# Attention's values as a seventh group of the mixers, second sums by adding transfers, one projection woven in

## The chip, the cores and the metric

The kernel runs on one core of a Trainium2 chip. The metric is the device time of one execution in microseconds (us); lower is better. The core's engines each run a queue of instructions in order: TensorE (PE: matmuls; PEld: its weight loads), VectorE (DVE), ScalarE (ACT), GpSimd (POOL) and SyncE (SP). SP, ACT and POOL also issue the transfers (DMAs).

## The reference

An encoder block over 256 tokens, width 2048, all in float32: a half-step gated FFN, then two token mixers in parallel, merged by gates, then a second half-step FFN and a norm. The part that matters here:

```python
h = rmsnorm(x, norm_mix_g[l])
proj = h @ w_in[l]
q_a, k_a, v_a, q_r, k_r, v_r, g_r, gate_a, gate_r = jnp.split(proj, IN_SPLIT_POINTS, axis=-1)
att = chunked_band_attention(q_a, k_a, v_a, rel_bias[l])       # 8 heads of 128, softmax
branch_a = att @ w_out_att[l]
ret = chunkwise_retention(rotary(q_r), rotary(k_r), v_r)       # 8 heads of 128, decay
branch_r = (silu(g_r) * ret) @ w_out_ret[l]
merged = sigmoid(gate_a) * branch_a + sigmoid(gate_r) * branch_r
x = x + merged @ w_out[l]
```

(The reshapes to heads are left out.) q_a, k_a, v_a, q_r, k_r, v_r and g_r are 1024 wide, the two gates 2048.

## The kernel before

**Matmuls.** Every product of activations and weights is made of three matmuls. Weights come as blocks of 256 rows by 512 columns in float32 (`raw`, 512 KB, on SP's queue). `split` makes a high part of a block on ScalarE (L140) and a low part on VectorE (L141); `three` multiplies high by high (L151), by the activations' low part (L152) and low by high (L154). Four pairs of split tiles go round, so a block's split can start when TensorE is through with the block four steps earlier.

**Steps.** The program is one list of steps; a step splits one block and multiplies it. A *standard* step (S below) serves both halves of the 256 tokens: 2 row pieces x 2 halves x 3 = 12 matmuls. A projection of 512 columns is 8 of them. `run` writes the instructions of all engines step by step; splits are written up to four steps ahead, and `later(n, fn)` puts other work n steps on. Each engine then keeps the order in which it was written.

**Groups.** The class `Strassen` makes two blocks of 512 columns at once with seven products instead of eight, from sums of blocks of the weights and of the activations. A group is 28 steps of 6 matmuls, in phases 0 to 3; for each of four row blocks jc there is a step r of a block itself and a step s of a sum (phase 3 has s only). A step's tiles are named by group, phase, jc and kind: `hiz49502s` is the high part of group z495, phase 0, jc 2, the sum. The order of the steps is 0r0 0r1 0s0 0r2 0s1 0r3 0s2 0s3 in phase 0, the same in phases 1 and 2, then 3s0 to 3s3.

The sums of weights live in two tiles per jc, `k` (kept) and `x`, both loaded on POOL's queue (L540). The *first* sum x + k is made on VectorE (L529); with `MIX_ADDED = (0,)` that of jc 0 is made by an adding transfer from k to x (L545) in all groups of the mixers but the first. The *second* sum adds the raw block of phase 1 to x, on VectorE in the step 1r (L597). The *third* replaces k by x - k on VectorE (L583), and x gets another block of weights added by a transfer from memory on POOL's queue (L584). That queue carries, in this order, the next group's loads, the third sums of this one, and so on, and each third sum waits until x has been split and k replaced.

**The mixers.** `weave` puts standard steps between the steps of the groups, at a rate worked out from their number and the shares in `MIX_SHARE`. The groups are attention's queries (`qa`, z390), the gates in four groups, and retention's gate (`gr`, z565); the projections woven in are attention's keys KA and values VA and retention's values VR, two each. Queries, keys and values go to memory and are brought back for the heads (`bring_back`). After the last group, at step `mixed`, follow the standard steps of retention's QR0, KR0, QR1 and KR1; the eight heads of attention are put between them at `HEAD_AT`, and retention's heads after each KR. Then branch a's and branch r's output projections, `w_out`, and the second FFN.

`ret_qk_done` takes QR or KR from its banks (ACT, tile `qr`), rotates it on VectorE in six operations per half of the tokens (`turn`, L905 to L908), transposes it on TensorE (`qr0p`, L368) and copies it out. `ROTATED` says how many steps after the projection's last step the two transposes stand.

Of the kernel before, what the change touches and what calls it, by code (L numbers as in the profile page):

```python
# [41 lines left out]
RET_WAIT = (14, 6)  # L42
RET_PUT = ((3, 5), (2, 2))
HELD = 6
MIX_ADDED = (0,)
FIRST_ADDED = (2, 3)
MIX_AHEAD = 12
FIRST_WAIT = 4
LAST_SUM = 24
ROTATED = {("q", 0): (6, 7), ("k", 0): (5, 6), ("q", 1): (4, 5), ("k", 1): (3, 4)}  # L50
HEAD_AT = (3, 6, 10, 13, 17, 20, 24, 27)

MIX_SHARE = (0.5,) * 4 + (1.0,) * 4 + (0.0,) * 4 + (0.2,) * 4
SHARE = (0.75,) * 4 + (1.0,) * 4 + (0.0,) * 4 + (0.2,) * 4
# [32 lines left out]
def block_kernel(ctx: ExitStack, tc: tile.TileContext, x, g1, w1g, w1u, w1d, gm, w_in, rel, woa, wor, wo,  # L87
# [419 lines left out]
    class Strassen:  # L507
# [3 lines left out]

        def __init__(self, norm, w1, col1, w2, col2, evict, added=()):
            self.added, self.summed = added, set()
            self.add_wait, self.early = ADD_WAIT, False
            self.norm, self.w, self.col, self.evict = norm, (w1, w2), (col1, col2), evict
            self.x, self.kept, self.acc, self.wide = {}, {}, {}, {}
            self.name = f"z{len(steps)}"
# [52 lines left out]
        def step(self, phase, jc, of_sum):  # L570
# [4 lines left out]
            def load():  # L575
                made["raw"] = weights_tile(f"raw{name}")
                i = 2 - phase
                fetch(made["raw"], self.w[i], self.rows(1, jc), self.col[i])

            def third():  # L580

                x, k = self.x[jc], self.kept[jc]
                nc.vector.tensor_sub(k, x, k)  # L583
                nc.gpsimd.dma_start(x, chunk(self.w[0], self.rows(1, jc), self.col[0]), accum_op=ALU.add)  # L584

            def prep():
                x = self.x[jc]
                if not of_sum:
                    if phase == 0:
                        made["w"] = split(self.kept[jc], name)  # L590
                        if jc not in self.added and not self.early:
                            self.first_once(jc)
                        return
                    raw = made.pop("raw")
                    made["w"] = split(raw, name)
                    if phase == 1:
                        nc.vector.tensor_add(x, x, raw)  # L597
                elif phase == 2:
                    made["w"] = split(self.kept.pop(jc), name)
                elif phase == 3:  # L600
                    made["w"] = split(self.x.pop(jc), name)
                else:
                    if phase == 0:
                        self.first_once(jc)
                    made["w"] = split(x, name)
                    if phase == 1:
                        third()

# [77 lines left out]
    def weave(jobs, apart, groups, lead, share, start=None, extra=0, ahead=8):  # L686
# [18 lines left out]
        for _ in range(lead):  # L705
            next_standard()
        seconds = []
        rate = (len(queue) - apart) / (len(groups) * sum(share))
        credit = 0.0
        first = max(len(steps) - ahead, D // NB)  # L710
        for n, (b, make) in enumerate(groups.items()):
            group = make()
            group.added = FIRST_ADDED if n == 0 and start is not None else group.added[:n]
            if n == 0 and start is not None:
                group.add_wait = 2
            group.early = n == 0 and ahead > 8
            loads = group.loads()
            if start is not None and n == 0:
                loads[0] = lambda load=loads[0]: [start(), load()]
            kept.extend((first + i if n == 0 else 0, fn) for i, fn in enumerate(loads))  # L720
            for i, part in enumerate(group.steps()):
                if i == HALF_K // KC + 2:
                    seconds.append(len(steps))
                steps.extend(part)
                credit += rate * share[i]
                if i + 1 == len(share):
                    at_hand[b] = len(steps) + 7

                turn = i + 1 == 3 * (HALF_K // KC)
                if (turn or credit >= (0.2 if (i + 1) % (HALF_K // KC) == 0 else 0.6)) and next_standard():  # L730
                    credit -= 1
# [159 lines left out]
    def ret_qk_done(key, b, after=None):  # L891
        def done(acc):
            srcs = []
            half = HD // 2

            def turn(t, s):
                r = tmp_tile(f"{key}{b}{t}r", "qk", 4)
                u = tmp_tile(f"{key}{b}{t}u", "scaled", 1)
                s4 = s.rearrange("p (h j d) -> p h j d", h=4, j=2)
                r4 = r.rearrange("p (h j d) -> p h j d", h=4, j=2)  # L900
                u4 = u.rearrange("p (h j d) -> p h j d", h=4, j=2)
                c = cos_sb[:, t, :].unsqueeze(1).to_broadcast([P, 4, half])
                n = sin_sb[:, t, :].unsqueeze(1).to_broadcast([P, 4, half])
                for j in range(2):
                    nc.vector.tensor_mul(r4[:, :, j, :], s4[:, :, j, :], c)  # L905
                    nc.vector.tensor_mul(u4[:, :, j, :], s4[:, :, 1 - j, :], n)
                nc.vector.tensor_sub(r4[:, :, 0, :], r4[:, :, 0, :], u4[:, :, 0, :])
                nc.vector.tensor_add(r4[:, :, 1, :], r4[:, :, 1, :], u4[:, :, 1, :])  # L908
                srcs.append(r)


            for t in range(NT):
                s = tmp_tile(f"{key}{b}{t}", "gate", 2)
                nc.scalar.activation(s, acc[t], AF.Copy, scale=nm.scale(t))
                later(1 + t, lambda t=t, s=s: turn(t, s))
            to_transposed(key, b, srcs, ROTATED[key[0], b])
            if after is not None:
                after()

        return done  # L920
# [17 lines left out]
    def attention(h):  # L938
# [53 lines left out]
            hi, lo = att.alloc(b)  # L992
            split_out(ps[:, :SEQ], hi[:, i, :], lo[:, i, :])

        return (0, scores), (1, powers), (2, shares), (4, transposes), (6 + (h < HEADS - 2), values)

    def all_attention():
        for h in range(HEADS):
# [77 lines left out]
    def gates(col1, col2, func, dsts):  # L1076


        def evict(t, side, r):
            if side == 1:  # L1080
                nc.scalar.activation(r, r, func)
            else:
                bank, r = r, tmp_tile(f"sg{col1}{t}", "gate", 2)
                nc.scalar.activation(r, bank, func, scale=nm.scale(t))
# [10 lines left out]
    def queries():  # L1095
# [9 lines left out]

        return Strassen(nm, w_in0, QA, w_in0, QA + NB, evict, MIX_ADDED)

    groups = {"qa": queries, **groups}
    weave(
        [proj(KA + b * NB, att_qk_done("ka", b), both) for b in range(2)]  # L1110
        + [proj(VA + b * NB, nat_done("va", b, AF.Copy), both) for b in range(2)]
        + [proj(VR + b * NB, nat_done("vr", b, AF.Copy), both) for b in range(2)],
        0, groups, MIX_LEAD, MIX_SHARE, None, EXTRA, MIX_AHEAD,
    )
    mixed = len(steps)
    for b in range(2):
        add([proj(QR + b * NB, ret_qk_done("qr", b)), proj(KR + b * NB, ret_qk_done("kr", b, lambda b=b: retention(b)))])

    merged = Operand("mg", D // NB)
    def load_gates(name, src):  # L1120
# [129 lines left out]
    mix = next(c for c, s in enumerate(steps) if s.job.w is w_in0)  # L1250
    at(mix - 18, load_rel)
    at(mix - 18, lambda: later(4, load_gain(gm, 1)))
    at(mixed - 6, set_bias)
    at(mixed - 3, lambda: bring_back(0))
    at(mixed + 5, lambda: bring_back(1))
    at(mixed, all_attention)
    at(merges[0][0] + 4, lambda: later(9, load_gain(g2, 2)))
    at(mixed + 16, load_ret_gates)
    at(mixed + 20, set_decay)
    for step, fn in merges:  # L1260
        at(step - 8, fn)

# [63 lines left out]
```

## Time and profile before

| what | value |
|---|---|
| median of 3 runs | 2037.34 us (2037.06 to 2037.85) |
| the profiled execution | 2037.64 us, its span 2035.9 us |
| TensorE busy | 99% |
| VectorE, ScalarE, GpSimd busy | 88%, 74%, 17% |
| moved by DMA | 504.77 MB, mean 248 GB/s |

Busy means that an instruction of the engine was under way. The mixers' groups run from 708 to 1054 us, the standard steps with the heads from there to 1159, the second FFN's first group starts at 1380 us. In lists of groups of instructions each row has line, engine, operation, tiles written and read, shape, count, and busy time; in timelines a row begins with its start and its length.

### The profile page before, as it was taken

What the parts mean: (1) busy time and instruction counts of PE and PEld (TensorE: products, weight loads), DVE (VectorE), ACT (ScalarE), POOL (GpSimd) and SP (SyncE); (2) the same over time, 40 slices, a digit from 0 to 9 for tenths busy, and PEclk for the clock granted to TensorE, in tenths of its full rate; (3) what the DMA queues carried; (4) which work ended last, traced back from release to release, by engine and by line L of the source; (5) the groups of instructions that cost most, each with busy time, mean ns of one, the idle gap of its engine ahead of it and who ended that gap; (6) DMA issues with size and microseconds to landing.
All of it is one profiled execution on the core that took longest, in us unless ns stands there. A gap on an engine that the chain in (4) does not pass through costs nothing.

```text
span 2035.9 us, 26220 instructions
## 1 busy us (share of the span) xinstructions
PE 2023.9 (99%) x9170; PEld 1678.8 (82%) x9170; DVE 1786.5 (88%) x1823; ACT 1504.3 (74%) x1886; POOL 342.9 (17%) x399
## 2 busy tenths in 40 slices
PE   9999999999999999999999999999999999999998
PEld 7788888888888888888888888888888888888886
DVE  7999999999998898999987677569999999999996
ACT  7788888878888777777765434557788888888885
POOL 1221122212112021111120000011112221122200
PEclk9999999999999999999999999999999999999999
DMA  9888899988878689899897645576889988889974
GB/s 311 255 249 258 255 269 281 262 240 250 260 235 237 218 232 303 273 283 286 256 320 236 209 156 185 186 247 188 263 268 276 274 243 237 258 269 270 285 199 135
DMA packets 226436, 504.77 MB, mean 248 GB/s; under 512 B 15776, under 2 KB 16480, under 8 KB 226304
## 3 DMA queue, kind: packets, MB, share of 16 engines
q1 hardware_dynamic: 154560, 297.31, 43.1%
q0 software_dynamic: 67536, 196.80, 37.4%
q10 hardware_dynamic: 4208, 8.99, 1.2%
q8 instruction: 72, 1.18, 0.2%
q14 instruction: 60, 0.49, 0.1%
HBM read 471.04 MB, written 10.50 MB: 237 GB/s over the span
## 4 chain that ended last, share of the span: by engine, by line
PE 98%; DVE 0%; DMA 0%; ACT 0%; issue 0%; POOL 0%; DVEq 0%; POOLq 0%; ACTq 0%; SPq 0%
PE acc L152 15%; PE acc L151 15%; PE acc L154 15%; DMA raw<-in_ffn_w_gate_dram 0%; PE z298a L152 0%; PE z530a L151 0%; PE z425a L151 0%; PE z850a L152 0%; PE z154a L152 0%; PE z1030a L152 0%; PE z994a L152 0%; PE z565a L151 0%; PE z742a L152 0%; PE z334a L152 0%; PE z118a L152 0%; PE z886a L152 0%
## 5 line engine op out<-in xcount | busy, mean ns | idle before, releaser
L141 DVE TENSOR_TENSOR lo<-raw,hi 128x1024 fp32r<-128x1024 f32 x351 | 427.7, 1221 | 118.7 <-ACT hi L140 113.8
L140 ACT CAST hi<-raw 128x1024 fp32r<-128x1024 f32 x351 | 368.0, 1050 | 178.0 <-PE acc L152 134.0
L808 ACT ACTIVATE xall<-acc 128x512 f32<-128x512 f32 x160 | 94.6, 591 | 13.4 <-PE acc L154 9.3
L805 ACT ACTIVATE acc<-xall 128x512 f32<-128x512 f32 x160 | 95.9, 600 | 2.5
L151 PE MATMUL acc<-hi,mgh 128*128 128x512 f32 x128 | 50.2, 392 | 0.0
L152 PE MATMUL acc<-hi,mgl 128*128 128x512 f32 x128 | 49.8, 389 | 0.0
L154 PE MATMUL acc<-lo,mgh 128*128 128x512 f32 x128 | 35.5, 390 | 0.0
L151 PE MATMUL acc<-hi,nma01h 128*128 128x512 f32 x80 | 32.0, 400 | 0.0
L151 PE MATMUL acc<-hi,nma00h 128*128 128x512 f32 x80 | 31.9, 398 | 0.0
L152 PE MATMUL acc<-hi,nma01l 128*128 128x512 f32 x80 | 31.2, 390 | 0.0
L152 PE MATMUL acc<-hi,nma00l 128*128 128x512 f32 x80 | 31.2, 390 | 0.0
L151 PE MATMUL acc<-hi,nma11h 128*128 128x512 f32 x80 | 31.2, 390 | 0.0
L151 PE MATMUL acc<-hi,nma10h 128*128 128x512 f32 x80 | 31.2, 390 | 0.0
L152 PE MATMUL acc<-hi,nma11l 128*128 128x512 f32 x80 | 31.2, 390 | 0.0
L152 PE MATMUL acc<-hi,nma10l 128*128 128x512 f32 x80 | 31.2, 390 | 0.0
L154 PEld LDWEIGHTS acc<-lo,mgh 128*128 128x128 f32 x128 | 24.0, 188 | 5.0
L151 PEld LDWEIGHTS acc<-hi,mgh 128*128 128x128 f32 x128 | 24.0, 188 | 4.9
L152 PEld LDWEIGHTS acc<-hi,mgl 128*128 128x128 f32 x128 | 24.1, 188 | 4.8
L151 PE MATMUL acc<-hi,atth 128*128 128x512 f32 x64 | 25.7, 402 | 0.0
L151 PE MATMUL acc<-hi,reth 128*128 128x512 f32 x64 | 25.3, 395 | 0.0
L359 POOL TENSOR_TENSOR n2rstd<-v,mhalf 128x2 f32<-128x2 f32 x1 | 0.7, 695 | 144.6 <-DVE v L358 144.6
L152 PE MATMUL acc<-hi,attl 128*128 128x512 f32 x64 | 25.0, 390 | 0.0
(6885 smaller groups left out, 7279.9 us busy)
## 6 DMA issues: line engine op xcount, KB each, us to landing
raw<-in_ffn_w_down_dram SPq DMA_DIRECT2D x176, 512.0 KB, 7.1
raw<-in_w_in_dram SPq DMA_DIRECT2D x80, 512.0 KB, 5.7
raw<-in_w_out_dram SPq DMA_DIRECT2D x32, 512.0 KB, 3.7
raw<-in_ffn_w_up_dram SPq DMA_DIRECT2D x16, 512.0 KB, 4.9
raw<-in_w_out_att_dram SPq DMA_DIRECT2D x16, 512.0 KB, 3.9
raw<-in_w_out_ret_dram SPq DMA_DIRECT2D x16, 512.0 KB, 3.7
raw<-in_ffn_w_gate_dram SPq DMA_DIRECT2D x15, 512.0 KB, 4.9
z390x<-in_w_in_dram POOLq DMA_DIRECT2D x8, 512.0 KB, 8.8
```

The lines of the kernel that those rows point to most:

```text
L140: nc.scalar.copy(hi, raw)
L141: nc.vector.tensor_sub(lo, raw, hi.bitcast(F32))
L151: nc.tensor.matmul(acc, ahi, whi, start=first, stop=False, **more)
L152: nc.tensor.matmul(acc, alo, whi, start=False, stop=False, **more)
L154: nc.tensor.matmul(acc, ahi, wlo, start=False, stop=last, **more)
L359: nc.gpsimd.tensor_tensor(dst, v, mhalf[:, :width], op=ALU.pow)
L805: nc.scalar.activation(acc, xs[t][:, cols], AF.Copy, scale=2.0)
L808: nc.scalar.activation(xs[t][:, cols], acc, AF.Copy, scale=0.5)
```

## The change

1. Attention's values become a group of the mixers, after the queries (`va`, z425): VA's two projections leave the list of standard steps, and the group's results go to memory half by half.
2. The second sums of jc 1 to 3 of every group of the mixers are made by adding transfers from memory on POOL's queue (`second`, L582 of the new file), after the sum's split in phase 0, ahead of the third sums. The one of jc 0 stays on VectorE.
3. The first sum of jc 0 is made on VectorE in all groups of the mixers (`MIX_ADDED = ()`).
4. QR0 is woven in as the last projection; after the mixers follow KR0, QR1 and KR1 only. The first group gets half as many standard steps again as the others (`fuller`).
5. The heads stand closer (`HEAD_AT`), the transposes of QR and KR at other steps (`ROTATED`), the rotations in another order and with a tile of their own, and the loads that go with them at other steps.

```diff
-MIX_ADDED = (0,)
+MIX_ADDED = ()
+SECOND_WAIT = 1
-ROTATED = {("q", 0): (6, 7), ("k", 0): (5, 6), ("q", 1): (4, 5), ("k", 1): (3, 4)}
-HEAD_AT = (3, 6, 10, 13, 17, 20, 24, 27)
+ROTATED = {("q", 0): (3, 4), ("k", 0): (4, 7), ("q", 1): (4, 7), ("k", 1): (3, 4)}
+HEAD_AT = (1, 4, 6, 9, 12, 14, 17, 20)
...
+            def second():
+                nc.gpsimd.dma_start(self.x[jc], chunk(self.w[1], self.rows(1, jc), self.col[1]), accum_op=ALU.add)
...
-                    if phase == 1:
+                    if phase == 1 and jc not in self.seconds:
                         nc.vector.tensor_add(x, x, raw)
...
                     made["w"] = split(x, name)
+                    if phase == 0 and jc in self.seconds:
+                        later(SECOND_WAIT, second)
...
-        rate = (len(queue) - apart) / (len(groups) * sum(share))
+        fuller = 0.5 if ahead > 8 else 0.0
+        rate = (len(queue) - apart) / ((len(groups) + fuller) * sum(share))
...
+            if ahead > 8:
+                group.seconds = range(1, HALF_K // KC)
...
-                for j in range(2):
+                for j, op in enumerate((ALU.subtract, ALU.add)):
+                    u = tmp.tile([P, NB // 2], F32, tag="turned", name=f"{key}{b}{t}u{j}", bufs=1)
                     nc.vector.tensor_mul(r4[:, :, j, :], s4[:, :, j, :], c)
-                    nc.vector.tensor_mul(u4[:, :, j, :], s4[:, :, 1 - j, :], n)
-                nc.vector.tensor_sub(r4[:, :, 0, :], r4[:, :, 0, :], u4[:, :, 0, :])
-                nc.vector.tensor_add(r4[:, :, 1, :], r4[:, :, 1, :], u4[:, :, 1, :])
+                    nc.vector.tensor_mul(u3, s4[:, :, 1 - j, :], n)
+                    nc.vector.tensor_tensor(r4[:, :, j, :], r4[:, :, j, :], u3, op=op)
...
-    groups = {"qa": queries, **groups}
+    def va_values():
+        return gates(VA, VA + NB, AF.Copy, [by_tokens(to_dram["va"][b]) for b in range(2)])
+
+    groups = {"qa": queries, "va": va_values, **groups}
     weave(
         [proj(KA + b * NB, att_qk_done("ka", b), both) for b in range(2)]
-        + [proj(VA + b * NB, nat_done("va", b, AF.Copy), both) for b in range(2)]
-        + [proj(VR + b * NB, nat_done("vr", b, AF.Copy), both) for b in range(2)],
+        + [proj(VR + b * NB, nat_done("vr", b, AF.Copy), both) for b in range(2)]
+        + [proj(QR, ret_qk_done("qr", 0), both)],
         0, groups, MIX_LEAD, MIX_SHARE, None, EXTRA, MIX_AHEAD,
     )
```

In the program, the groups of the mixers are z390, z425, z460, z495, z530 and z565 before, with 7 standard steps in each; they are z390, z425, z458, z491, z523, z556 and z588 after, with 7, 5, 5, 4, 5, 4 and 4. In phase 0 the last five have no standard step before the end of the phase; before, one stood after 0r2 and one after 0s3.

**Start of a group on VectorE.** Phase 0 of the fourth group before (`lo499` is a standard step's low part; L529 a first sum):

```order
L141 TENSOR_TENSOR loz49500r_7815<-z495k0_7305,hiz49500r_7814 128x1024
L141 TENSOR_TENSOR loz49501r_7825<-z495k1_7665,hiz49501r_7824 128x1024
L529 TENSOR_TENSOR z495x1_7696<-z495x1_7696,z495k1_7665 128x1024
L141 TENSOR_TENSOR loz49500s_7838<-z495x0_7323,hiz49500s_7837 128x1024
L141 TENSOR_TENSOR loz49502r_7848<-z495k2_7722,hiz49502r_7847 128x1024
L529 TENSOR_TENSOR z495x2_7734<-z495x2_7734,z495k2_7722 128x1024
L141 TENSOR_TENSOR lo499_7863<-raw499_7639,hi499_7862 128x1024
L141 TENSOR_TENSOR loz49501s_7875<-z495x1_7696,hiz49501s_7874 128x1024
L141 TENSOR_TENSOR loz49503r_7887<-z495k3_7758,hiz49503r_7886 128x1024
L529 TENSOR_TENSOR z495x3_7770<-z495x3_7770,z495k3_7758 128x1024
L141 TENSOR_TENSOR loz49502s_7898<-z495x2_7734,hiz49502s_7897 128x1024
```

and of the fourth group after (L142 is the low part, L530 the first sum):

```order
L142 TENSOR_TENSOR loz49100r_7734<-z491k0_7267,hiz49100r_7733 128x1024
L530 TENSOR_TENSOR z491x0_7285<-z491x0_7285,z491k0_7267 128x1024
L142 TENSOR_TENSOR loz49101r_7745<-z491k1_7584,hiz49101r_7744 128x1024
L530 TENSOR_TENSOR z491x1_7615<-z491x1_7615,z491k1_7584 128x1024
L142 TENSOR_TENSOR loz49100s_7758<-z491x0_7285,hiz49100s_7757 128x1024
L142 TENSOR_TENSOR loz49102r_7768<-z491k2_7641,hiz49102r_7767 128x1024
L530 TENSOR_TENSOR z491x2_7653<-z491x2_7653,z491k2_7641 128x1024
L142 TENSOR_TENSOR loz49101s_7783<-z491x1_7615,hiz49101s_7782 128x1024
L142 TENSOR_TENSOR loz49103r_7793<-z491k3_7677,hiz49103r_7792 128x1024
L530 TENSOR_TENSOR z491x3_7689<-z491x3_7689,z491k3_7677 128x1024
L142 TENSOR_TENSOR loz49102s_7806<-z491x2_7653,hiz49102s_7805 128x1024
```

The standard step's low part is gone, and a first sum of jc 0 stands in the second place.

**QR0's rotation on VectorE, after.** Phase 2 of the last group (L654 is the group's combination of two banks, `qr00` and `qr01` the two halves of QR0, L914 to L916 the rotations):

```order
L142 TENSOR_TENSOR loz58822r_9332<-rawz58822r_9216,hiz58822r_9331 128x1024
L654 SCALAR_TENSOR_TENSOR z588c12_9308<-z588c_9088,nmminus_92,z588c12_9308 128x512
L914 TENSOR_TENSOR qr00r_9338<-qr00_9326,cos_sb_80 128x4x64
L915 TENSOR_TENSOR qr00u0_9339<-qr00_9326,sin_sb_81 128x256
L916 TENSOR_TENSOR qr00r_9338<-qr00r_9338,qr00u0_9339 128x4x64
L914 TENSOR_TENSOR qr00r_9338<-qr00_9326,cos_sb_80 128x4x64
L915 TENSOR_TENSOR qr00u1_9343<-qr00_9326,sin_sb_81 128x256
L916 TENSOR_TENSOR qr00r_9338<-qr00r_9338,qr00u1_9343 128x4x64
L142 TENSOR_TENSOR loz58821s_9354<-z588k1_8878,hiz58821s_9353 128x1024
L914 TENSOR_TENSOR qr01r_9357<-qr01_9328,cos_sb_80 128x4x64
```

and the same place on TensorE (L155 is a product with a low part, `acc90` QR0's banks, L369 the transposes):

```order
L155 MATMUL acc90_1_8745<-lo607_9267,nma11h_6114 128x512 x2
L155 MATMUL z588b_9129<-loz58820r_9285,nma01h_6110 128x512 x2
L155 MATMUL z588b_9129<-loz58821r_9297,nma01h_6110 128x512 x2
L369 MATMUL qr0p0_9378<-id_sb_78,qr00r_9338 128x128 x4
L155 MATMUL z588a_9065<-loz58820s_9311,nms7h_6366 128x512 x2
L369 MATMUL qr0p1_9396<-id_sb_78,qr01r_9357 128x128 x4
L155 MATMUL z588b_9129<-loz58822r_9332,nma01h_6110 128x512 x2
```

(The products with high parts between these rows are left out.) Between QR0's last matmul and the first transposes stand two steps of a group, 2r0 and 2r1, and one more between the transposes. Before, they stood behind standard steps of KR0, six and seven steps after QR0's last.

**POOL's queue**, from a group's third sums to the next group's, before (L545 is the first sum of jc 0 by transfer):

```order
L540 DMA z530x0_7805<-in_w_in_dram 128x2x512
L545 DMA z530x0_7805<-z530k0_7787 128x1024
L584 DMA z495x0_7323<-in_w_in_dram 128x2x512
L584 DMA z495x1_7696<-in_w_in_dram 128x2x512
L584 DMA z495x2_7734<-in_w_in_dram 128x2x512
L584 DMA z495x3_7770<-in_w_in_dram 128x2x512
```

and after (L582 the second sums, L588 the third):

```order
L541 DMA z523x0_7724<-in_w_in_dram 128x2x512
L582 DMA z491x1_7615<-in_w_in_dram 128x2x512
L582 DMA z491x2_7653<-in_w_in_dram 128x2x512
L582 DMA z491x3_7689<-in_w_in_dram 128x2x512
L588 DMA z491x0_7285<-in_w_in_dram 128x2x512
L588 DMA z491x1_7615<-in_w_in_dram 128x2x512
L588 DMA z491x2_7653<-in_w_in_dram 128x2x512
L588 DMA z491x3_7689<-in_w_in_dram 128x2x512
```

Seven adding transfers stand where five stood.

More of the change, by code (lines that the diff above doesn't have):

```diff
@@ L513, in __init__ @@
             self.added, self.summed = added, set()
-            self.add_wait, self.early = ADD_WAIT, False
+            self.add_wait, self.early, self.seconds = ADD_WAIT, False, ()
             self.norm, self.w, self.col, self.evict = norm, (w1, w2), (col1, col2), evict
@@ L724, in weave @@
                 steps.extend(part)
-                credit += rate * share[i]
+                credit += rate * share[i] * (1 + (fuller if n == 0 else 0))
                 if i + 1 == len(share):
@@ L897, in turn @@
                 r = tmp_tile(f"{key}{b}{t}r", "qk", 4)
-                u = tmp_tile(f"{key}{b}{t}u", "scaled", 1)
                 s4 = s.rearrange("p (h j d) -> p h j d", h=4, j=2)
                 r4 = r.rearrange("p (h j d) -> p h j d", h=4, j=2)
-                u4 = u.rearrange("p (h j d) -> p h j d", h=4, j=2)
                 c = cos_sb[:, t, :].unsqueeze(1).to_broadcast([P, 4, half])
                 n = sin_sb[:, t, :].unsqueeze(1).to_broadcast([P, 4, half])
-                for j in range(2):
+                for j, op in enumerate((ALU.subtract, ALU.add)):
+                    u = tmp.tile([P, NB // 2], F32, tag="turned", name=f"{key}{b}{t}u{j}", bufs=1)
+                    u3 = u.rearrange("p (h d) -> p h d", h=4)
                     nc.vector.tensor_mul(r4[:, :, j, :], s4[:, :, j, :], c)
-                    nc.vector.tensor_mul(u4[:, :, j, :], s4[:, :, 1 - j, :], n)
-                nc.vector.tensor_sub(r4[:, :, 0, :], r4[:, :, 0, :], u4[:, :, 0, :])
-                nc.vector.tensor_add(r4[:, :, 1, :], r4[:, :, 1, :], u4[:, :, 1, :])
+                    nc.vector.tensor_mul(u3, s4[:, :, 1 - j, :], n)
+                    nc.vector.tensor_tensor(r4[:, :, j, :], r4[:, :, j, :], u3, op=op)
                 srcs.append(r)
@@ L993, in values @@
             split_out(ps[:, :SEQ], hi[:, i, :], lo[:, i, :])
-        return (0, scores), (1, powers), (2, shares), (4, transposes), (6 + (h < HEADS - 2), values)
+        return (0, scores), (1, powers), (2, shares), (4, transposes), (6, values)
     def all_attention():
@@ L1080, in evict @@
             if side == 1:
-                nc.scalar.activation(r, r, func)
+                if func != AF.Copy:
+                    nc.scalar.activation(r, r, func)
             else:
@@ L1116, in block_kernel @@
     for b in range(2):
-        add([proj(QR + b * NB, ret_qk_done("qr", b)), proj(KR + b * NB, ret_qk_done("kr", b, lambda b=b: retention(b)))])
+        jobs = [proj(QR + b * NB, ret_qk_done("qr", b)), proj(KR + b * NB, ret_qk_done("kr", b, lambda b=b: retention(b)))]
+        add(jobs if b else jobs[1:])
     merged = Operand("mg", D // NB)
@@ L1252, in block_kernel @@
     at(mix - 18, lambda: later(4, load_gain(gm, 1)))
-    at(mixed - 6, set_bias)
-    at(mixed - 3, lambda: bring_back(0))
-    at(mixed + 5, lambda: bring_back(1))
+    at(mixed - 8, set_bias)
+    at(mixed - 6, lambda: bring_back(0))
+    at(mixed + 2, lambda: bring_back(1))
     at(mixed, all_attention)
     at(merges[0][0] + 4, lambda: later(9, load_gain(g2, 2)))
-    at(mixed + 16, load_ret_gates)
-    at(mixed + 20, set_decay)
+    at(mixed + 12, load_ret_gates)
+    at(mixed + 14, set_decay)
     for step, fn in merges:
```

## The prediction

> **What bounds the kernel now.** I read the page first: the busy times and the chain that ended last.
>
> ```profile
> span 2035.9 us, 26220 instructions
> PE 2023.9 (99%) x9170; PEld 1678.8 (82%) x9170; DVE 1786.5 (88%) x1823; ACT 1504.3 (74%) x1886; POOL 342.9 (17%) x399
> PE 98%; DVE 0%; DMA 0%; ACT 0%; issue 0%; POOL 0%; DVEq 0%; POOLq 0%; ACTq 0%; SPq 0%
> ```
>
> TensorE is the chain. So a matmul removed is worth its own pace, and every new wait of TensorE costs its full length. The pace comes from the timeline of one mixer group (z495, the fourth), whose first matmul and the next group's first are
>
> ```profile
> 883.26 0.39 PE L151 MATMUL z495a<-hiz49500r,nma00h 128*128 128x512 f32 x1
> 940.38 0.39 PE L151 MATMUL z530a<-hiz53000r,nma00h 128*128 128x512 f32 x1
> ```
>
> The 0.39 us is how long one takes, not how often one starts: between the rows lie 28 group steps of 6 matmuls and 7 standard steps of 12, that is 252, in 57.12 us. One starts every 0.2267 us; a group step is 1.36 us, a standard step 2.72 us. Nothing is left in those 57 us for a wait.
>
> Who could make TensorE wait is read from the windows (second number of each pair in brackets: instructions; last two columns: share of the DMA engines, GB/s) and from the waits.
>
> ```profile
> 883.20:940.40 57.20, 57.20 (x254) 47.35 (x254) 54.25 (x49) 41.83 (x46) 11.60 (x13) 1.00 0.92 281
> 860.00:880.00 20.00, 20.00 (x90) 16.57 (x89) 17.79 (x17) 15.72 (x17) 7.05 (x9) 1.00 1.06 348
> 1020.00:1040.00 20.00, 20.00 (x90) 16.57 (x89) 20.00 (x19) 12.97 (x13) 7.82 (x10) 1.00 1.03 247
> 1040.00:1060.00 20.00, 20.00 (x90) 16.58 (x89) 13.77 (x13) 15.41 (x19) 0.53 (x1) 1.00 1.04 396
> ACT hi L140 <- PE acc L152: 134.0, 87, 3.9
> DVE lo L141 <- ACT hi L140: 113.8, 99, 3.8
> ```
>
> In a group VectorE is busy 54.25 of 57.20 us and the DMA engines 0.92. ScalarE (41.83 us) has room: its largest idle is the wait for TensorE to free one of the four split slots. Both others are near their limit, and the change takes standard steps, which relieve them, out of every group but the first.
>
> **The matmuls.** Two standard projections are 2 x 8 steps x 12 = 192 matmuls; one group is 28 x 6 = 168. 24 fewer at 0.2267 us: **-5.44 us**. That needs TensorE fed as now.
>
> **VectorE at the start of a group.** The second sums of blocks 1 to 3 move off VectorE; the first sum of block 0, which POOL's queue added before, moves onto it. Over a group that fits: the last five groups have 4.4 standard steps on average, so 4 first sums, 1 second sum, 4 operations for the third and 32.4 low parts are 41.4 operations of 1.135 us (below), with two narrow ones 48.3 us, against 28 x 1.36 + 4.4 x 2.72 = 50.1 us of TensorE. But in these five the first eight steps have no standard step among them any more. These rows of z495 give the margin there:
>
> ```profile
> 880.07 1.22 DVE L141 TENSOR_TENSOR loz49500r<-z495k,hiz49500r 128x1024 fp32r<-128x1024 f32 x1
> 882.52 1.22 DVE L529 TENSOR_TENSOR z495x<-z495x,z495k 128x1024 f32<-128x1024 f32 x1
> 891.60 1.22 DVE L141 TENSOR_TENSOR loz49502s<-z495x,hiz49502s 128x1024 fp32r<-128x1024 f32 x1
> 884.17 0.61 PE L154 MATMUL z495a<-loz49500r,nma00h 128*128 128x512 f32 x2
> 895.05 0.61 PE L154 MATMUL z495c<-loz49502s,nms5h 128*128 128x512 f32 x2
> ```
>
> Eight operations from 882.52 to 891.60: 1.135 us each. The first low part ends at 881.29 and TensorE wants it at 884.17, 2.88 us later; at the seventh step 2.23 us are left. Up to that step VectorE has 10 operations in both kernels (11.35 us). Before, TensorE has 6 x 1.36 + 2.72 = 10.88 us for them: 2.88 + 10.88 - 11.35 = 2.41, against 2.23 measured. After, it has 8.16 us: 2.88 + 8.16 - 11.35 = -0.31. TensorE waits 0.31 us there. All five of z458, z491, z523, z556 and z588 have this order of VectorE up to the seventh step. Going on step by step (a group step gains 1.36 - 1.135, an extra add costs 1.135), z491, which has no standard step before block 0's second sum either, waits another 0.46 us at 1r1; z556 another 0.24 us at 1r3; the rest recover. Sum 5 x 0.31 + 0.70 = 2.25: **+2.25 us**. z425 has a standard step in time and loses nothing. Bounds: with the 0.18 us by which the check missed, 1.3 to 3.2 us.
>
> **The projection woven in.** QR0 now ends inside the last group (z588), and its rotated halves are transposed 3 and 4 steps later, where steps are of 1.36 us: TensorE reaches the first transposes 2.72 us after QR0's last matmul. Before, they were 6 and 7 steps away, among steps of 2.72 us. What has to happen in between, from before:
>
> ```profile
> 1078.13 0.39 PE L151 MATMUL acc<-hi,nma00h 128*128 128x512 f32 x1
> 1078.33 0.69 ACT L914 ACTIVATE qr<-acc,nmrstd 128x512 f32<-128x512 f32 x1 [0.69 <-PE acc L154]
> 1078.92 1.04 ACT L140 CAST hi<-raw 128x1024 fp32r<-128x1024 f32 x1
> 866.04 0.75 DVE L648 SCALAR_TENSOR_TENSOR z460c<-z460c,nmminus,z460c 128x512 f32<-128x512 f32 x1
> 866.70 1.22 DVE L141 TENSOR_TENSOR loz46021s<-z460k,hiz46021s 128x1024 fp32r<-128x1024 f32 x1
> 1081.79 0.42 DVE L905 TENSOR_TENSOR qr00r<-qr,cos_sb 128x256 f32<-128x256 f32 x1
> 1083.81 1.22 DVE L141 TENSOR_TENSOR lo<-raw,hi 128x1024 fp32r<-128x1024 f32 x1
> 1094.72 0.60 PE L368 MATMUL qr0p<-id_sb,qr00r 128*128 128x128 f32 x4
> 1095.07 0.48 PE L151 MATMUL acc<-hi,nma00h 128*128 128x512 f32 x1
> ```
>
> The second half leaves its bank from 0.20 us after the last matmul and takes 0.59 us of ScalarE; then comes the split of 2r2, whose slot the same matmul frees (1.05), its low part on VectorE (1.135), the group's combination (866.04 to 866.70: 0.66) and six rotations (1081.79 to 1083.81: 2.02): 5.66 us in a row, so the first transposes wait 2.9 us. They take 0.35 us and 2s0 1.36, which ends at 7.4 us; but VectorE has another low part and six rotations to do, until 8.8: the second transposes wait 1.4 us. **+4.4 us.** In the new order the last of each three rotations reads what the one just ahead wrote, which no row of before shows; I take nothing for it. Bounds: eviction and rotations alone make 2.8 us, a first wait of 0.1 and a second of 1.4; with 0.4 us more for each half it is 5.2: 1.5 to 5.2 us. What is late next: the copies of the transposes queue on ScalarE ahead of the split of 2s2, which TensorE reaches two steps later.
>
> **The transfers.** From 846 to 862 us POOL's queue (q0) moved only third sums, which add, and SP's (q1) only plain blocks:
>
> ```profile
> q1 hardware_dynamic: 1399, 2.70, 44.3%
> q0 software_dynamic: 544, 1.05, 39.9%
> z460x<-in_w_in_dram POOLq DMA_DIRECT2D x4, 512.0 KB, 7.2
> z495k<-in_w_in_dram POOLq DMA_DIRECT2D x1, 512.0 KB, 10.9
> ka0back<-ka0d POOLq DMA_DIRECT2D x1, 512.0 KB, 16.0
> ```
>
> A transfer is 0.524 MB: two adding ones took 39.9% of 16 us, 3.2 us each of the 16 engines; 5.15 plain ones 44.3%, 1.38 us each. A group before has 25 plain (23, and gate writes that make 2) and 5 adding, 50.5 us; its row above says 0.92 x 57.2 = 52.6. After: 22.4 plain and 7 adding, 53.3 us, in 50.1 us of TensorE. Full windows show a share of 1.03 to 1.06, so 53.3 us pass in 51. Bounds: at 1.32 us for a plain one (396 GB/s) and in proportion 3.05, 50.9 and so no loss; with the 2 us that the check missed added, 55.4 us, 53 us a group, 2.9 us more than TensorE needs. Over six groups 0 to 17 us. The middle prices give 0.9 us a group, 5.4 in six, of which VectorE's waits, counted above, cover 2.25. I take **+2 us**, nearer to nothing: 29.4 transfers in 50.1 us are 308 GB/s, and the row nearest in kind (860 to 880: third sums, loads and raw blocks together) moved 348. The second sums are in time: z491 has eight group steps and a standard step, 13.6 us, between the split of a block and its next, and third sums landed after 7.2.
>
> The Trainium skill (DMA: Bandwidth & Descriptors, Specifications) gives a limit of about 358 GB/s of HBM per core. By it the 308 GB/s would pass and this term would be zero; the 396 GB/s above are more than that limit, and the page prices no transfer that adds, so the bounds from the rows stand.
>
> **At no cost.** The values' way out: a group's evictions and four writes of 256 KB in place of two projections' evictions and two of 512 KB, on ScalarE, which was idle for 57.2 - 41.8 us of a group and, with 2.6 splits of 1.05 us fewer in 50.1 us, still is for 11. Heads closer: 24 standard steps instead of 32 follow the mixers, with this load before:
>
> ```profile
> 1054.60:1159.20 104.60, 104.60 (x507) 88.02 (x506) 72.96 (x150) 55.79 (x92) 6.84 (x13) 1.00 0.73 244
> ```
>
> VectorE loses 8 splits and 4.0 us of rotations there, which leaves 59.9 us of 82: the cover stays. Without it branch a's first block would be late next; from the last head's values to their use it has one standard step, where it had two. The first heads' operands are issued after the last third sum and landed after 16 us; some 25 us lie ahead of their use.
>
> **Sum.** -5.44 + 2.25 + 4.4 + 2 = +3.2 us on the profiled execution's 2037.64 us (1.7 us above its span, 0.3 above the median): 2040.5 us against the median of 2037.34.
>
> **Rivals.** (1) The gain comes through: both waits at the transposes under 0.5 us and VectorE's under 0.4 make 2032 to 2033.3. For it: TensorE waits for nothing in these 57 us, so ScalarE and VectorE may run ahead of my order. Against it: both waits are sums of serial rows, and the check on z495 missed by 0.18 us only. It decides below 1.4 us of new waits. Chance 0.18. (2) The DMA engines become the bound of the six later groups: with 10 us instead of 2, 2048.5. For it: the share goes from 0.92 to 1.06 at equal prices. Against it: the 348 GB/s. It decides from about 3 us on. Chance 0.34. (3) The forecast, waits of VectorE and at the transposes, 2034 to 2041.4: 0.48.
>
> A difference of 0.2% (4.1 us) is about what a measurement here can tell from none. Below 2033.3 only rival 1 lies: faster 0.18. Between lies the forecast: same 0.48. Rival 2, and transfers a little dearer than taken, are slower: 0.34. The range reaches from rival 1's lower end to rival 2's price, 2032 to 2048.5; what it leaves out is mainly transfers dearer still, toward the 17 us.
>
> **What the changed profile would show.** TensorE idle twice around `qr0p`, 3 and 1.3 us, ended by VectorE; short idle before low parts at the seventh step of z458 to z588, and no gap on VectorE there; DMA share at 1.0 or more over the later groups. If idle of ScalarE or VectorE ended by DMA stands in those groups, rival 2 is right; if `qr0p` waits for nothing, my order of events there is wrong.

## The result and the profile after

The changed kernel takes 2050.43 us (median of 4 runs, 2050.21 to 2050.5) against 2037.49 us before: ratio 1.0064, 95% interval 1.0051 to 1.0076, 12.9 us slower. That is outside the predicted range (2032 to 2048.5) and 10 us above the predicted 2040.5. The profiled execution took 2050.36 us. One execution in experiment 1 (5301 us) and one in experiment 7 (2250 us) were far longer than the others, and the ratios leave them out.

The page of the changed kernel: its span, TensorE's busy time, and the shares of the chain that ended last.

```profile
span 2048.6 us, 26275 instructions
PE 2025.5 (99%) x9146; PEld 1673.7 (82%) x9146; DVE 1800.1 (88%) x1833; ACT 1515.7 (74%) x1900; POOL 374.4 (18%) x427
PE 94%; DVE 3%; ACT 1%; DMA 1%; issue 1%; POOL 0%; DVEq 0%; ACTq 0%; POOLq 0%; SPq 0%
```

TensorE's share of the chain fell from 98% to 94%; VectorE, ScalarE and transfers now stand in it. Where, is read from the first matmul of each group and of branch a (`atth`). TensorE's timeline, before (two rows) and after:

```profile
708.33 0.39 PE L151 MATMUL z390a<-hiz39000r,nma00h 128*128 128x512 f32 x1
1159.24 0.39 PE L151 MATMUL acc<-hi,atth 128*128 128x512 f32 x1
```

```profile
708.16 0.39 PE L152 MATMUL z390a<-hiz39000r,nma00h 128*128 128x512 f32 x1
...
766.18 0.39 PE L152 MATMUL z425a<-hiz42500r,nma00h 128*128 128x512 f32 x1
...
821.65 0.39 PE L152 MATMUL z458a<-hiz45800r,nma00h 128*128 128x512 f32 x1
...
875.04 0.39 PE L152 MATMUL z491a<-hiz49100r,nma00h 128*128 128x512 f32 x1
...
929.35 0.39 PE L152 MATMUL z523a<-hiz52300r,nma00h 128*128 128x512 f32 x1
...
981.55 0.39 PE L152 MATMUL z556a<-hiz55600r,nma00h 128*128 128x512 f32 x1
...
1033.01 0.39 PE L152 MATMUL z588a<-hiz58800r,nma00h 128*128 128x512 f32 x1
...
1172.04 0.48 PE L152 MATMUL acc<-hi,atth 128*128 128x512 f32 x1
```

From the mixers' start to branch a it was 450.91 us and is 463.88, 12.97 more; from there to the end of the span nothing changed (876.7 and 876.6 us). 24 matmuls are gone (5.44 us), so 18.4 us of waits are new. By group, the length less its matmuls at 0.2267 us (and, in z425, less 2.7 us of transposes, which stood there before too): z425 1.1, z458 1.7, z491 5.3, z523 0.5, z556 2.5, and 7.3 from z588 on. Who ended them is said by TensorE's waits in that stretch (total, times, longest); before, the same view has no row:

```profile
PE qr0p L369 <- DVE qr00r L916: 3.3, 1, 3.3
PE z491c L152 <- ACT z491s L648: 1.8, 1, 1.8
PE qr0p L369 <- DVE qr01r L916: 1.4, 1, 1.4
PE z588a L152 <- ACT z588c L662: 1.0, 1, 1.0
PE z425c L152 <- ACT z425s L648: 0.8, 1, 0.8
PE z458a L152 <- ACT hiz45822s L141: 0.5, 1, 0.5
PE z491c L155 <- DVE loz49101s L142: 0.4, 1, 0.4
PE z556c L155 <- DVE loz55601s L142: 0.4, 1, 0.4
PE z556c L155 <- DVE loz55602s L142: 0.4, 1, 0.4
PE z491c L155 <- DVE loz49102s L142: 0.4, 1, 0.4
PE z556c L155 <- DVE loz55613r L142: 0.3, 1, 0.3
PE z588c L155 <- DVE loz58802s L142: 0.3, 1, 0.3
PE z523c L155 <- DVE loz52302s L142: 0.2, 1, 0.2
PE z458c L155 <- DVE loz45802s L142: 0.2, 1, 0.2
PE z556c L155 <- DVE loz55600s L142: 0.2, 1, 0.2
```

A wait costs some 0.2 to 0.3 us more than its row says (the matmuls right behind it start further apart). Measured from start to start, the rows make five sums: transposes (`qr0p`) 5.0 us; evictions that TensorE waits for at the border of two phases (`z491s`, `z425s`, `z588c`) 4.4; low parts and so VectorE 5.4; the split of 2s2 in z458 1.1; and a stretch at half the clock behind the wait of z491 1.6, shown at the end. The prediction had the first and the third, and the fourth as a part of its term for the transfers; the second and the fifth were not in it.

**The border of two phases.** Phase 1 goes on in bank c, where phase 0 stopped, so the copy `z491s` of the bank must be out first. ScalarE and TensorE there, after:

```profile
884.47 1.05 ACT L141 CAST hiz49103s<-z491x 128x1024 fp32r<-128x1024 f32 x1 [2.35 <-DVE z491x L530]
887.83 1.04 ACT L141 CAST hi<-raw 128x1024 fp32r<-128x1024 f32 x1
888.78 0.68 ACT L648 ACTIVATE z491s<-z491c,nmminus 128x512 f32<-128x512 f32 x1
887.06 0.61 PE L155 MATMUL z491c<-loz49103s,nms5h 128*128 128x512 f32 x2
889.51 0.50 PE L152 MATMUL z491c<-hiz49110r,nms3h 128*128 128x512 f32 x1 [1.83 <-ACT z491s L648]
```

and at the same border of the fourth group before:

```profile
897.07 0.69 ACT L642 ACTIVATE z495s<-z495c,nmminus 128x512 f32<-128x512 f32 x1 [0.23 <-PE z495c L154]
896.87 0.39 PE L151 MATMUL acc<-hi,nma00h 128*128 128x512 f32 x1
899.58 0.39 PE L151 MATMUL z495c<-hiz49510r,nms3h 128*128 128x512 f32 x1
```

Before, a standard step stands at the border: 2.71 us of other matmuls, from 896.87 to 899.58, in which the eviction (897.07 to 897.76) is done and over. After, z425 and z491 have none there, nor has z588 between phases 2 and 3, and just these three pay. In z491 it is worse since ScalarE has splits in its queue ahead of the eviction, late themselves: the split of 0s3 waited 2.35 us for a first sum (L530).

### The profile page after: what moved, and what is told of

The parts are those of the page before. It is cut to its first block, busy times and chain, and to the rows that moved or that the text cites. A ratio compares the mean times of both kernels' runs of the same rounds, so it can differ in the third digit from the quotient of the medians.

```text
span 2048.6 us, 26275 instructions
## 1 busy us (share of the span) xinstructions
PE 2025.5 (99%) x9146; PEld 1673.7 (82%) x9146; DVE 1800.1 (88%) x1833; ACT 1515.7 (74%) x1900; POOL 374.4 (18%) x427
## 4 chain that ended last, share of the span: by engine, by line
PE 94%; DVE 3%; ACT 1%; DMA 1%; issue 1%; POOL 0%; DVEq 0%; ACTq 0%; POOLq 0%; SPq 0%
PE acc L152 15%; PE acc L155 15%; PE acc L153 15%; DMA rawz45823r<-in_w_in_dram 1%; PE z425a L152 0%; PE z190a L152 0%; PE z118a L152 0%; PE z898a L152 0%; PE z425a L153 0%; PE z334a L153 0%; PE z82a L153 0%; PE z1042a L152 0%; PE z754a L152 0%; PE z154a L153 0%; PE z826a L153 0%
## 5 line engine op out<-in xcount | busy, mean ns | idle before, releaser
L142 DVE TENSOR_TENSOR lo<-raw,hi 128x1024 fp32r<-128x1024 f32 x335 | 407.9, 1220 | 109.3 <-ACT hi L141 104.7
L141 ACT CAST hi<-raw 128x1024 fp32r<-128x1024 f32 x335 | 351.4, 1051 | 170.9 <-PE acc L153 137.4
L155 PE MATMUL acc<-lo,mgh 128*128 128x512 f32 x128 | 35.5, 389 | 0.0
L155 PEld LDWEIGHTS acc<-lo,mgh 128*128 128x128 f32 x128 | 24.0, 188 | 5.0
L152 PE MATMUL acc<-hi,nma00h 128*128 128x512 f32 x64 | 26.0, 407 | 0.0
L152 PE MATMUL acc<-hi,nma01h 128*128 128x512 f32 x64 | 25.9, 405 | 0.0
L153 PE MATMUL acc<-hi,nma01l 128*128 128x512 f32 x64 | 25.0, 391 | 0.0
L153 PE MATMUL acc<-hi,nma00l 128*128 128x512 f32 x64 | 25.0, 391 | 0.0
L152 PE MATMUL acc<-hi,nma10h 128*128 128x512 f32 x64 | 25.0, 390 | 0.0
L153 PE MATMUL acc<-hi,nma10l 128*128 128x512 f32 x64 | 25.0, 390 | 0.0
L152 PE MATMUL acc<-hi,nma11h 128*128 128x512 f32 x64 | 24.9, 390 | 0.0
L153 PE MATMUL acc<-hi,nma11l 128*128 128x512 f32 x64 | 24.9, 390 | 0.0
```

The lines of the kernel that those rows point to most:

```text
L141: nc.scalar.copy(hi, raw)
L142: nc.vector.tensor_sub(lo, raw, hi.bitcast(F32))
L152: nc.tensor.matmul(acc, ahi, whi, start=first, stop=False, **more)
L153: nc.tensor.matmul(acc, alo, whi, start=False, stop=False, **more)
L155: nc.tensor.matmul(acc, ahi, wlo, start=False, stop=last, **more)
```

## Experiments

Theory A: the loss is the sum of such separate waits, which come from where the standard steps (and QR0's transposes) stand. Theory B: the DMA engines are the bound, the prediction's rival 2. All ratios are to the kernel before, whose median was 2037.37 to 2037.59 us in these runs.

**1. The transposes later.**

```diff
-ROTATED = {("q", 0): (3, 4), ...
+ROTATED = {("q", 0): (8, 9), ...
```

> QR0's two transposes stand 8 and 9 steps after its last step instead of 3 and 4; nothing else differs from the changed kernel (2050.43). Theory A (the loss is a sum of separate waits of TensorE: transposes 5.0 us, evictions at the borders of phases that have no standard step 4.2, VectorE in phase 0 4.9, the clock's dip after the longest wait 1.6, one late third sum 1.1): both waits at the transposes (3.42 and 1.55 us) go, and with them perhaps the 1.17 us before phase 3, so 2044.2 to 2045.6. Theory B (the DMA engines are the bound and every wait is their work that comes late): TensorE arrives 5 us earlier at blocks that come no earlier and waits there, 2048 or more.

2047.3 us, ratio 1.0044 (1.0030 to 1.0058): 3.1 us less than the changed kernel, where A said 5 to 6; its runs lie between 2044.7 and 2047.7 us, so the size is rough. Some 1.6 of the 3.1 us are the clock, which did not fall behind z491's wait in this execution; z588 gave 2.3, and z458 lost 0.6. The waits of TensorE in z588 show where the rest went:

```profile
PE z588b L155 <- DVE loz58823r L142: 1.7, 1, 1.7
PE z588a L155 <- DVE loz58821s L142: 0.7, 1, 0.7
PE z588a L152 <- ACT z588c L662: 0.6, 1, 0.6
```

The rotations still stand on VectorE between the low parts of group steps; TensorE now waits for the low parts behind them instead of for the transposes. Moving the one who waits takes only part of the time away; the 4 us of VectorE have to lie where there is room.

**2. The price of adding.**

```diff
-nc.gpsimd.dma_start(self.x[jc], chunk(self.w[1], ...), accum_op=ALU.add)
+nc.gpsimd.dma_start(self.x[jc], chunk(self.w[1], ...))
```

> The second sums' transfers of block 1 to 3 copy instead of adding (the sum is left out): same places, same bytes from memory, same waits, but each moves at a plain transfer's price, 1.4 us of the 16 engines instead of 3.2; 5.4 us less in each of seven groups. Theory A: only the late third sum of z458 (1.1 us) and a little of VectorE's lateness at the start of z491 and z556 go: 2047 to 2049.5. Theory B: everything in the six later groups goes but the two evictions and the transposes, some 8 to 11 us: 2039.5 to 2042.5.

2048.36 us, ratio 1.0054 (1.0041 to 1.0066): 2.1 us less. The wait for z458's 2s2 is gone, and one of z491's low parts; transposes, borders and the other low parts stand (its waits have `z491s` 1.8, `z425s` 0.8 and `qr0p` 3.3 again). The clock fell behind the transposes here, which made z588 some 1.8 us longer, instead of behind z491's border (1.6), so the two about cancel. Theory B's 8 to 11 us are not there.

**3. More standard steps in phase 0.**

```diff
-MIX_SHARE = (0.5,) * 4 + (1.0,) * 4 + (0.0,) * 4 + (0.2,) * 4
+MIX_SHARE = (1.0,) * 4 + (0.5,) * 4 + (0.0,) * 4 + (0.2,) * 4
```

> Of the standard steps of a group more stand in phase 0 and fewer in phase 1 (MIX_SHARE 1.0 and 0.5 instead of 0.5 and 1.0): every group has one behind 0s3 and one or two inside phase 0; as many matmuls and transfers as before. Theory A: the evictions at the border of phases 0 and 1 (0.94 and 1.99 us) and the clock's dip (1.6) go, and most of VectorE's 4.9 us in phase 0; something comes back in phase 1, where VectorE then has the third sums without them: 2041 to 2045. Theory B: no transfer is saved, 2048.5 to 2051.5.

2042.45 us, ratio 1.0025 (1.0015 to 1.0036): 8.0 us less, with every matmul and every transfer kept. Both borders of phases 0 and 1 and the slow clock are gone. What its view of waits still shows is z588's (transposes 3.3 and 1.4, `z588c` 1.0, since its last border is still without a standard step) and 1.4 us of VectorE. Theory B falls.

**4. A first sum less on VectorE.**

```diff
-                        if jc not in self.added and not self.early:
+                        if jc not in self.added and not self.early and not (jc == 0 and self.seconds):
                             self.first_once(jc)
...
-                    if phase == 0:
+                    if phase == 0 and not (jc == 0 and self.seconds and not self.early):
                         self.first_once(jc)
```

> The first sum of block 0 is left out in the six groups after the first (VectorE saves 1.135 us in phase 0 of each; the transfers are the same). Theory A: VectorE's waits in phase 0 go (0.48 in z458, 1.5 in z491, 0.47 in z523, 1.76 in z556, 0.55 in z588), and part of the eviction and of the clock's dip in z491 behind them (1 to 3.6): 2042 to 2045. Theory B: 2049 to 2050.5, since the transfers set the pace.

2045.07 us, ratio 1.0037 (1.0023 to 1.0050): 5.4 us less. Of VectorE's waits two in z556 are left (0.4 and 0.3); the border of z491 still costs 1.8 and the clock's dip with it. So the phase-0 waits were VectorE's, and the border's wait does not go with them. (Its split of 0s3 still waits 2.35 us for a first sum, that of jc 3.) The wait for z458's 2s2 is gone too, with every transfer kept.

**5. An even spread.** Five standard steps in each group, at every border that needs one; QR0's rotations and transposes behind the last group.

```diff
-MIX_LEAD = 6
+MIX_LEAD = 5
-MIX_SHARE = (0.5,) * 4 + (1.0,) * 4 + ...
+MIX_SHARE = (0.5,) * 4 + (0.5,) * 4 + ...
-        fuller = 0.5 if ahead > 8 else 0.0
+        fuller = 0.0
-ROTATED = {("q", 0): (3, 4), ...
+ROTATED = {("q", 0): (8, 9), ...
-                later(1 + t, lambda t=t, s=s: turn(t, s))
+                later((4 if (key, b) == ("qr", 0) else 1) + t, lambda t=t, s=s: turn(t, s))
```

> The changed kernel with its standard steps spread evenly: five in each of the seven groups (one less ahead of the mixers, none extra in the first group, MIX_SHARE 0.5 and 0.5), behind 0r2, 0s3, 1r1, 1r3 and 2s3 in each; QR0 so ends behind 2s3 of the last group, its rotations are written four and five steps on, its transposes eight and nine. Matmuls and transfers are those of the changed kernel. Theory A: no border without a standard step where a bank is taken over, VectorE in phase 0 has a standard step in time, rotations and transposes are among steps of 2.72 us: nearly all of the 18 us of waits go, 2033 to 2037 (2032.0 is the time before less 24 matmuls). Theory B: as many bytes in the same time of TensorE, 2043 or more.

2037.85 us, ratio 1.0002 (0.9993 to 1.0011): 12.6 us less than the changed kernel, and the time of before, 0.9 us above what A allowed. Two waits are left, and the longer has ScalarE's rows

```profile
1071.88 0.69 ACT L922 ACTIVATE qr<-acc,nmrstd 128x512 f32<-128x512 f32 x1 [4.31 <-DMA gr<-sg]
1072.46 1.03 ACT L141 CAST hiz58733s<-z587x 128x1024 fp32r<-128x1024 f32 x1
```

QR0's second half needs a buffer that is still being written to memory as a gate (`gr<-sg`); ScalarE stands 4.3 us, the split of 3s3 with it, and TensorE 2.5. The groups ahead of that run without a wait while the DMA engines are full (windows as in the prediction):

```profile
917.20:968.90 51.70, 51.70 (x229) 42.80 (x229) 49.76 (x45) 38.17 (x42) 14.27 (x15) 1.00 1.05 309
```

A share of 1.05, 309 GB/s, seven adding transfers, and 228 matmuls in 51.7 us, which is 0.2267 us each. In this order of the steps the transfers of the change pass in TensorE's own time.

**6. The rotations at once.** As 5, but with the rotations one and two steps behind QR0's end, in phase 3.

```diff
-                later((4 if (key, b) == ("qr", 0) else 1) + t, lambda t=t, s=s: turn(t, s))
+                later(1 + t, lambda t=t, s=s: turn(t, s))
```

> The evenly spread kernel, but QR0's rotations are written one and two steps after its end, in phase 3 of the last group, instead of four and five, among the standard steps behind it. Theory A: the 4 us of rotations lie between low parts of group steps, which take 1.135 us of VectorE in 1.36 us of TensorE, so TensorE waits 1 to 2.5 us longer than in the evenly spread kernel. Theory B: no difference (within 0.5 us).

2040.05 us, ratio 1.0014 (1.0006 to 1.0023): 2.2 us more than 5, as A has it; TensorE waits 1.4 us more for a low part (`lo`) behind the rotations. Part of the rest is the clock: from 1075.2 to 1082 us its mean is 0.50 here and 0.75 in 5.

**7. Part 2 alone, on the kernel before, adding and copying.** Values as standard steps, QR0 behind the mixers, the old tables; in the second kernel the transfers copy.

```diff
 # against the kernel before
+    if phase == 0 and jc in self.seconds:
+        later(SECOND_WAIT, second)
...
-    if phase == 1:
+    if phase == 1 and jc not in self.seconds:
         nc.vector.tensor_add(x, x, raw)
```

> Part 2 of the change alone on the kernel before: second sums of blocks 1 to 3 by adding transfers, everything else as before (values as standard steps, seven standard steps in each of six groups, first sum of block 0 by transfer, QR0 behind the mixers, old places of heads and transposes; only the order of the rotations is the new one). Eight adding transfers stand in a group instead of five. Theory A: VectorE has three operations less and no border is bare: 2037 to 2039. Theory B: 9.6 us more of the 16 engines in a group of 57.1 us that had 52.6 makes them the bound: 2042 to 2065.

> Part 2 alone on the kernel before, with the second sums' transfers copying instead of adding (the sum is left out): the places and waits in the queue are the same, each of the three takes 1.4 us of the 16 engines instead of 3.2. Theory A2 (the 4.2 us that part 2 alone cost are the price of adding: DMA engines full, third sums and blocks late): 2037 to 2038. Theory B2 (they are POOL's queue, which waits for the split of 0s1 with the third sums behind it): 2040.5 to 2042.

Adding: 2041.66 us, ratio 1.0019 (1.0010 to 1.0028), 4.2 us slower than before: A was wrong here, by 2.7 us, and the lowest that B allowed was missed by 0.3. Copying: 2037.29 us, ratio 0.9999 (0.9991 to 1.0008). So it is the price of adding and not POOL's queue. ScalarE's waits for blocks, and the window of the fourth group, adding:

```profile
ACT hi L141 <- DMA raw<-in_w_in_dram: 15.1, 10, 2.9
887.00:944.00 57.00, 57.00 (x253) 47.22 (x252) 50.97 (x46) 41.37 (x46) 15.21 (x16) 1.00 1.04 308
```

and copying:

```profile
ACT hi L141 <- DMA raw<-in_w_in_dram: 7.0, 6, 2.1
883.00:940.00 57.00, 57.00 (x253) 47.23 (x252) 50.99 (x46) 41.72 (x46) 13.82 (x16) 1.00 1.00 319
```

With eight adding transfers beside 25 plain ones the engines are full over four groups and blocks come late; TensorE waits in three of them. Here, on its own, rival 2's mechanism is real. The change gives back 2.6 plain transfers and one adding one per group. By the prediction's prices that leaves a group of experiment 5 (23 plain, 7 adding: 54.1 us in 51.7) hardly less full than one here (25 and 8: 60.1 us in 57.1), so why experiment 5 has no such wait is not shown.

**8. Part 1 alone, on the kernel before.** The values as a seventh group; second sums on VectorE, first sum of block 0 by transfer, QR0 behind the mixers.

```diff
 # against the changed kernel
-                group.seconds = range(1, HALF_K // KC)
+                group.seconds = ()
-MIX_ADDED = ()
+MIX_ADDED = (0,)
-        + [proj(QR, ret_qk_done("qr", 0), both)],
 ...
```

> Part 1 alone on the kernel before: attention's values as a seventh group, so 26 standard steps in seven groups; second sums on VectorE, first sum of block 0 by transfer, QR0 behind the mixers, old places of heads and transposes. 24 matmuls less than before, no adding transfer more in a group. Theory A: VectorE has 49.8 us of work in 48.2 us of TensorE in a group, some 1.6 us a group in the six later groups, and two borders of phases 0 and 1 and one of 2 and 3 are bare (some 4 us): 2042 to 2049. Theory B: 2031.5 to 2034.5.

2058.68 us, ratio 1.0104 (1.0090 to 1.0118): 21 us slower than before, where A allowed 11.5. The longest waits and the window of its fifth group:

```profile
PE z423c L152 <- ACT z423s L648: 2.9, 1, 2.9
PE z518c L152 <- ACT z518s L648: 2.7, 1, 2.7
PE z581a L152 <- ACT z581c L662: 1.6, 1, 1.6
920.20:971.40 51.20, 48.46 (x205) 39.30 (x204) 49.17 (x45) 37.22 (x42) 11.59 (x13) 0.97 0.89 268
```

The DMA engines have room (0.89) and VectorE has 49.17 of 51.2 us: with fewer standard steps and the second sums still on it, VectorE is the bound, and four borders are without a standard step. From start to start, TensorE's waits for low parts make some 14 us, those at the four borders 9, and the slow clock behind one of them 1.6. In this order of the steps part 1 needs part 2's relief of VectorE; part 1 alone with the even spread was not run.

**9. The even spread, its two waits taken away.**

```diff
 # against 5
-LAST_SUM = 24
+LAST_SUM = 20
-                s = tmp_tile(f"{key}{b}{t}", "gate", 2)
+                s = tmp_tile(f"{key}{b}{t}", *(("qk", 4) if (key, b, t) == ("qr", 0, 0) else ("gate", 2)))
```

> The evenly spread kernel with its two remaining waits taken away: the first half of QR0 leaves its bank into another buffer (the one that it took was still being written to memory for the gates, and ScalarE stood 4.3 us behind it, TensorE 2.6 us and some 1.4 us more at a lower clock), and the activations' last sum is made four steps earlier (TensorE waited 1.16 us for it in the first group). Theory A: 5.4 us of waits go, 2032.2 to 2034. Theory B: the transfers then are what TensorE arrives at, 2035.5 to 2038.

2033.61 us, ratio 0.9982 (0.9973 to 0.9991): 3.8 us faster than before and 16.8 faster than the changed kernel, by the same matmuls and transfers. One wait of TensorE is left in the stage, 0.5 us in a head; the fifth group (916.1 to 967.7 us) again has a DMA share of 1.04 and 309 GB/s without a wait.

**10. A standard step more in phase 0.** As 9, behind 0r2, 0r3, 0s3, 1r2 and 2s3.

```diff
-MIX_SHARE = (0.5,) * 4 + (0.5,) * 4 + ...
+MIX_SHARE = (0.0, 1.0, 1.0, 1.0) + (0.0, 1.0, 0.0, 0.0) + ...
```

> As the kernel with its own buffers, but the five standard steps of a group stand behind 0r2, 0r3, 0s3, 1r2 and 2s3, one more in phase 0 and one less in phase 1. Theory A: phase 1 has 13 operations of VectorE for 10.9 us of TensorE and one standard step instead of two; 0 to 1 us a group of waits there, 2032 to 2039. Theory B: the same as the kernel with its own buffers within 0.7 us.

2034.89 us, ratio 0.9988 (0.9979 to 0.9997), 1.3 us behind 9. Phase 1 did not begin to wait; its two waits are at the transposes of the queries (`qa0p`, 0.8) and in a head (0.7). It tells little between the theories; 9 stays the better.

## Why the prediction was wrong, step by step

- **The matmuls: right.** 24 fewer are 5.44 us, and where TensorE is fed (experiments 5 and 9) the groups run at 0.2267 us a matmul.
- **The step that failed: what the removed standard steps had been doing.** The prediction took them as 2.72 us of relief for VectorE and the DMA engines. They also cover the evictions at the borders of phases. It counted VectorE's operations across these borders, and noted that z491 has no standard step before block 0's second sum, but never asked what ScalarE had to do between the last matmul into a bank and the next; "at no cost" was said of ScalarE from its idle share. The missing term measured 4.4 us, and in this execution 1.6 us of slow clock followed its longest wait: 6.0 us, more than half of the miss of 9.9. All seven borders without a standard step in the changed kernel and in experiment 7 make TensorE wait, 0.8 to 2.9 us by their rows, and no border with one does; where experiments 3 and 5 put a step there, the wait is gone.
- **VectorE at the start of a group: right in kind, too small.** 2.25 us (1.3 to 3.2) were forecast, 5.4 came. The margin of 2.88 us was carried over from z495. In z458, z523 and z588 it is there (2.89, 2.89 and 2.77), and each loses some 0.5 us, nearly all at the seventh step, where the prediction put 0.31. In z491 and z556 it is not, and they lose 1.5 and 2.4:

```profile
872.95 1.22 DVE L142 TENSOR_TENSOR loz49100r<-z491k,hiz49100r 128x1024 fp32r<-128x1024 f32 x1
875.95 0.62 PE L155 MATMUL z491a<-loz49100r,nma00h 128*128 128x512 f32 x2
863.65 1.23 DVE L142 TENSOR_TENSOR loz45822s<-z458k,hiz45822s 128x1024 fp32r<-128x1024 f32 x1 [2.16 <-ACT hiz45822s L141]
976.31 0.69 ACT L935 ACTIVATE vr<-acc,nmrstd 128x512 f32<-128x512 f32 x1 [0.28 <-PE acc L155]
976.90 1.04 ACT L141 CAST hiz52333s<-z523x 128x1024 fp32r<-128x1024 f32 x1
979.71 1.22 DVE L142 TENSOR_TENSOR loz55600r<-z556k,hiz55600r 128x1024 fp32r<-128x1024 f32 x1
982.46 0.61 PE L155 MATMUL z556a<-loz55600r,nma00h 128*128 128x512 f32 x2
```

z491's first low part ends at 874.17 (start and 1.22) and is wanted at 875.95: 1.78 us, not 2.88. Most of what it lost came from the late split in z458 (third row): without the adding the margin is 2.50, and one of z491's two waits goes (experiment 2). z556's margin is 1.53 us, in experiment 2 as well. The rows ahead of it show ScalarE taking a half of VR, a projection that ends in z523, out of its bank before the split of 3s3; that this cost the margin is read from the rows and was not tested. Experiment 4 shows that the waits were VectorE's.
- **The transposes: right.** 4.4 us forecast, 5.0 measured, in the order of events that was written down. That the rotations cost VectorE and not only the one who waits for them is what experiment 1 added.
- **The transfers: near in size, but not by the mechanism.** 2 us were forecast, as time by which the transfers outlast TensorE in the later groups. What the trace has is one late split, in z458, 1.1 us, and that went in experiments 3 and 4 too, which kept every transfer; experiment 5 has a DMA share of 1.05 and no wait. That copying gives 2.1 is partly luck, since in it a slow stretch of the clock that went is made up by one that came. The prices are borne out by experiment 7: with eight adding transfers the share is 1.04 in the window shown and TensorE waits in three groups, and with the same bytes copied it is 1.00 and TensorE waits nowhere. Rival 2 named a time near the result, 2048.5 us, by a mechanism that experiments 3 and 5 refute in this place. Its sign in the prediction, idle of ScalarE ended by DMA in these groups, is there in the changed kernel, but in experiment 9 too, where TensorE waits for none of it; the longest for a block in each:

```profile
ACT hiz52313r L141 <- DMA rawz52313r<-in_w_in_dram: 2.4, 1, 2.4
ACT hiz52113r L141 <- DMA rawz52113r<-in_w_in_dram: 2.6, 1, 2.6
```

Neither that sign nor a high share tells of a bound by itself.
- **The heads closer: free, as said.** From branch a on the two executions are alike, and TensorE's waits have no row behind 1084 us.

The terms as measured make -5.4 + 5.4 + 4.4 + 1.6 + 5.0 + 1.1 = 12.1 of 12.9 us. The remaining 0.8 us was not traced. Against the forecast, 4.4 and 1.6 us were not counted, VectorE's term was 3.2 too small and the transposes' 0.6, and the transfers' was 0.9 too large.

## What to carry to other kernels

Before a piece of work is taken out of a stream, list everything that it covers, bank evictions between two matmuls into one bank among them, not only the engine that is nearly full. A margin read at one place holds for what stands ahead of it there; read it again for each group, and look for a late split or a projection that ends just before. Of one list of instructions, the order alone made 2050.4, 2042.5 or 2037.9 us, and 2033.6 with one tile in another buffer besides: where filler steps are few, put them where something must be waited for, evenly, and not where a rate happens to let them fall.

## What was not expected of the hardware

Behind z491's wait TensorE's clock fell to half for some 3.4 us (window of 890 to 894 us; 0.57 is the mean granted clock in it):

```profile
890.00:894.00 4.00, 4.00 (x13) 3.08 (x12) 4.00 (x5) 1.84 (x3) 0.00 (x0) 0.57 1.09 226
```

Matmuls started 0.43 us apart instead of 0.2267 there, which made a wait of 1.8 us cost 1.6 more. The idle time ahead of it was 1.83 us, with two waits of 0.4 us in the 8 us before. The Trainium skill (TensorE: Matmul & The Clock Gate, Part 1) lets the clock fall to half after an idle window of about 3.4 us; no idle time of that length stands ahead of this fall. The transposes' wait of 3.3 us in the same execution was not followed by it, while in experiments 2 and 4 it was; the same wait of 1.8 us at z491 was followed by it in experiment 4, and not in experiments 1 and 2. What decides it was not settled. The price of adding in a transfer to SBUF, by the prediction's rows 3.2 us of the 16 engines for 512 KB against 1.4, made 4.4 us between the two kernels of experiment 7.
